# A decoder trunk planned by list scheduling: a denser layout for a small recursion, a higher threshold for constant products, and new priorities

## The chip, the core and the metric

The kernel runs on one core of one Trainium2 chip. A core has five engines that run side by side, each with its own instruction queue: TensorE (PE, matrix products; its weight loads are shown as PEld), VectorE (DVE), ScalarE (ACT), GpSimd (POOL) and SyncE (SP), which issues the transfers. The clock that TensorE is granted varies during a run, and the profile shows it. The metric is the device time of one execution in microseconds, as a median of several runs.

## The reference

A trunk of two layers over 512 positions of width 1024. Each layer is

```python
h = rms_norm(x, attn_pre_norm[i])
z = h @ w_in[i]
y_attn = dilated_attention_mixer(aq, ak, av, positions)
y_conv = conformer_conv_mixer(conv_u, conv_dw[i], ...)
y_gdn = gated_deltanet_mixer(gdn_qkv, gdn_gate, gdn_a, gdn_b, ...)
mix = jnp.concatenate([y_attn, y_conv, y_gdn], axis=-1)
x = x + rms_norm(mix @ w_out[i], attn_post_norm[i])
h = rms_norm(x, ffn_pre_norm[i])
f = (jax.nn.silu(h @ w_gate[i]) * (h @ w_up[i])) @ w_down[i]
x = x + rms_norm(f, ffn_post_norm[i])
```

What matters here is the gated DeltaNet with four heads of width 128. It works in chunks and solves, in each, a unit lower triangular system:

```python
m = jnp.where(strict, jnp.einsum('bhncd,bhnsd->bhncs', k_beta, k) * decay, 0.0)
sol = lax.linalg.triangular_solve(m + jnp.eye(C), rhs, left_side=True, lower=True, unit_diagonal=True)
```

## The kernel before

Activations lie transposed, features on the 128 partitions and the 512 positions along the row. Every large product (`dense`, line 703) is float32 split into two parts of a faster format: high times high, high times low, low times high, so three products of 512 (or twice 256) columns for each 128 x 128 block of weights. The weights come through SP in units of four blocks (tile `wr`) and are split into `wh` (ACT) and `wl` (DVE or POOL). The results of all these products are called `pmm`. There are 1600 blocks in all.

A layer's mixer is written as segments in the order of `SEGMENTS` (line 30): K, Q and V project and convolve the DeltaNet's keys, queries and values; C0, C1 and CN are the convolution module; A and B0 to B3 the attention; S the scan over chunks; G0 to G3 the output gates. Segment K also holds the triangular inverse. It forms the matrices `em` (named `am` in the code) for four heads by four blocks of 128 positions, cuts out the 16 x 16 blocks on the diagonal (`abd`, `acm`), and inverts all of these at once by a recursion over 16 columns (line 1059). For that, `acm` is negated (`acn`), written to a scratch array in HBM and read back with each row spread over 16 partitions (`aext`). Column c then takes, for each of two halves of the 16 matrices, one DVE product of c + 1 rows by 8 matrices (`sbt`) and one DVE reduction into `pext`: 32 products and 32 reductions a layer. From `pext` the block diagonal inverse `P` is made for each head, transposed by DVE in blocks of 32 (`tm`), and then merged to blocks of 32, 64 and 128 by small TensorE products: `pc`, `pd` and `pt` in the profile, with results moved by ACT and DVE in between (tile `c`).

No order is written by hand. The program first records all operations, each with a cost from a table (`cost`, line 252). `Plan.forward` (line 399) then simulates the engines and picks, at each free engine, the ready operation with the highest rank: the length of the longest path to the end, plus the segment's entry in `BONUS` (line 127), and for the matrix products of `dense` also that in `DENSE` (line 128), both in ns. An operation waits in `fits` (line 438) until the buffers that it needs are free, with caps: 78 slots of 512 columns in SBUF, 7 banks in PSUM, and quotas for single names (8 for `z`, the projected tiles). When TensorE has nothing ready, line 542 looks at the last `TICK` (3.41 us): if less work than `TUNE["fill"]`, in columns, was done, a product of constants, 256 columns, is put into TensorE's queue (tile `fill`, issued through line 1368). `TUNE["low"]`, 2900 columns, is the limit below which the planner believes that the clock halves. The resulting order is issued as it stands, so each engine's queue is fixed when the program is built. Most instructions carry the line of the helper that issues them, 591, so the profile is read by tiles.

Of the kernel before, what the change touches and what calls it, by code (L numbers as in the profile page):

```python
# [9 lines left out]
F32 = mybir.dt.float32  # L10
F32R = mybir.dt.float32r
AF = mybir.ActivationFunctionType
OP = mybir.AluOpType
# [116 lines left out]
TUNE = {'spread': 2.8, 'low': 2900, 'fill': 4000, 'warm': 12, 'early': 0, 'hib': 2000.0, 'raw': 4, 'half': 12000.0, 'taps': 14, 'plo': 4, 'hold': 1000, 'passes': 0, 'S': 78, 'P': 7, 'Q': 5, 'ahead': 5, 'more': 6, 'n_out': 4, 'n_ffn': 6, 'n_down': 2, 'n_in': 8}  # L130
# [112 lines left out]
class Plan:  # L243
# [8 lines left out]
    def cost(self, op, eng, name, outs, ins, kw):  # L252
# [24 lines left out]
        if eng == "DVE":  # L277
# [121 lines left out]
    def forward(self):  # L399
# [50 lines left out]
        while events:  # L450
# [17 lines left out]
            for e in engines:  # L468
# [4 lines left out]
                while avail[e] and (e != "SP" or len(skipped) < 12):  # L473
# [17 lines left out]
                    break  # L491
                if chosen:
# [101 lines left out]
def trunk(nc, tc, xT, wst, wab, par, con, big, out, depth=DEPTH, dbg=None):  # L594
# [4 lines left out]
    with ExitStack() as ctx:  # L599
# [202 lines left out]
        def project_out(k_tiles, gain, n_cut):  # L802

            o = [slot([128, S], name=f"o{m}") for m in range(KD)]
            acc = slot([128, S], name="oacc")
# [632 lines left out]
```

## Time and profile before

| what | value |
|---|---|
| median of 3 runs | 1375.4 us (1375.05 to 1376.79) |
| the profiled execution | 1378.01 us |
| its span, first to last instruction | 1376.2 us |
| mean granted TensorE clock | 0.981 |
| PE busy | 1340.8 us, 97% |
| DVE busy | 824.9 us, 60% |
| ACT busy | 650.8 us, 47% |
| POOL busy | 176.3 us, 13% |
| constant products (fill) | 109 |

The page gives busy times by engine, and then the span in 40 equal slices of 34.4 us, a digit of tenths for each. A row of instructions names the engine, the operation, the tiles (written <- read), the shapes, the count, and the busy time with the mean of one in ns. Matrix products overlap in the pipeline, so the time that one takes in a stream is read from start to next start. The rows on which the argument rests are shown in the prediction.

### The profile page before, as it was taken

The page shows a single profiled execution, that of the slowest core. Times are in us where ns is not written, and L with a number is a line of the kernel's source. Part 1 is how long each engine was busy: PE and PEld are TensorE (multiplying, and loading weights), DVE is VectorE, ACT ScalarE, POOL GpSimd, SP SyncE. Part 2 cuts the span into 40 slices and gives each one's busy share as a digit, 9 for nine tenths or more (in the row PEclk, how much of TensorE's full clock was granted, in tenths as well). Part 3 has the DMA queues.
Part 4 walks back from the last instruction along what each step waited for, and adds up shares of the span by engine and source line. Part 5 has one row for each costly group of instructions (what it writes and reads, how often), then busy time and mean ns, then how long its engine had stood idle before and what let it go on. Part 6 is the DMA issues. An engine that isn't in the chain of part 4 may idle for free.

```text
span 1376.2 us, 20826 instructions
## 1 busy us (share of the span) xinstructions
PE 1340.8 (97%) x7645; PEld 1143.7 (83%) x7645; DVE 824.9 (60%) x1739; ACT 650.8 (47%) x1523; POOL 176.3 (13%) x138
## 2 busy tenths in 40 slices
PE   8999999999999999999999899999999999999996
PEld 7977886798888888888998788777898888888886
DVE  7599889675343335533788848774493444346324
ACT  5565598864232224333574546796562222244321
POOL 1045562000000000000003347310000000000000
PEclk9999999999999999999999869999999999999998
DMA  6234121413333331432304113222232332223311
GB/s 244 63 68 135 51 62 32 146 55 92 100 94 90 92 92 47 123 106 85 108 16 100 39 55 90 79 62 77 84 110 86 105 92 85 87 57 114 111 46 62
DMA packets 64438, 118.51 MB, mean 86 GB/s; under 512 B 8016, under 2 KB 8784, under 8 KB 64336
## 3 DMA queue, kind: packets, MB, share of 16 engines
q1 hardware_dynamic: 64336, 117.19, 28.2%
q8 instruction: 60, 0.98, 0.3%
q14 instruction: 42, 0.34, 0.1%
HBM read 112.70 MB, written 2.36 MB: 84 GB/s over the span
## 4 chain that ended last, share of the span: by engine, by line
PE 83%; DVE 7%; ACT 6%; DMA 2%; issue 1%; SPq 1%; DVEq 0%; ACTq 0%
PE pmm L591 72%; PE pas L591 1%; PE pd L591 1%; PE pc L591 1%; PE pao L591 1%; DVE sct L591 1%; DMA wr<-in_wst_dram 1%; DVE sbt L591 1%; PE fill L1368 1%; SPq L591 1%; DVE wl L591 1%; PE pss L591 1%; ACT L588 1%; PE pbc L591 1%; DVE pext L591 1%
## 5 line engine op out<-in xcount | busy, mean ns | idle before, releaser
L591 DVE TENSOR_TENSOR wl<-wr,wh 128x512 fp32r<-128x512 f32 x382 | 265.3, 728 | 73.4 <-ACT wh L591 54.6
L591 ACT CAST wh<-wr 128x512 fp32r<-128x512 f32 x400 | 226.9, 619 | 48.9 <-PE pmm L591 30.6
L591 ACT ACTIVATE g<-g 128x512 f32<-128x512 f32 (+1 forms) x50 | 28.4, 579 | 303.9 <-DVE g L591 303.9
L591 DVE TENSOR_TENSOR g<-pmm,rst 128x512 f32<-128x512 f32 (+1 forms) x50 | 31.0, 626 | 216.2 <-PE pmm L591 215.8
L591 PE MATMUL pmm<-gl,wh 128*128 128x512 f32 (+1 forms) x440 | 124.9, 347 | 0.0
L591 PE MATMUL pmm<-gh,wl 128*128 128x512 f32 (+1 forms) x280 | 92.5, 347 | 0.0
L591 PE MATMUL pmm<-gh,wh 128*128 128x512 f32 (+1 forms) x280 | 92.3, 348 | 0.0
L591 PEld LDWEIGHTS pmm<-gl,wh 128*128 128x128 f32 x440 | 71.3, 189 | 10.5 <-DVE gl L591 0.4
L591 POOL TENSOR_TENSOR ca<-ca,cm 128x510 f32<-128x510 f32 (+12 forms) x52 | 69.3, 1333 | 30.8 <-ACT cm L591 26.7
L591 POOL TENSOR_TENSOR abd<-em,cn 128x512 f32<-128x512 f32 x8 | 10.1, 1292 | 488.4 <-PE pbc L591 483.7
L591 ACT ACTIVATE osq<-pmm 128x256 f32<-128x256 f32 (+1 forms) x40 | 18.8, 470 | 106.4 <-PE pmm L591 104.2
L591 PE MATMUL pmm<-h0h,wh 128*128 128x512 f32 (+1 forms) x168 | 62.0, 370 | 6.6 <-ACT h0h L591 5.0
L591 DVE TENSOR_TENSOR g<-pmm,g 128x512 f32<-128x512 f32 (+1 forms) x50 | 31.1, 625 | 57.3 <-PE pmm L591 55.7
L591 DVE TENSOR_TENSOR oacc<-oacc,osq 128x256 f32<-128x256 f32 (+1 forms) x36 | 19.1, 539 | 74.5 <-ACT osq L591 74.5
L591 PE MATMUL pmm<-h0h,wl 128*128 128x512 f32 (+1 forms) x168 | 60.4, 360 | 1.4 <-DVE wl L591 1.4
L591 DVE SCALAR_TENSOR_TENSOR ca<-cy,pr,ca 128x495 f32<-128x495 f32 (+8 forms) x64 | 60.1, 940 | 1.7 <-ACT ca L591 1.0
L591 PE MATMUL pmm<-h0l,wh 128*128 128x512 f32 (+1 forms) x168 | 61.0, 363 | 0.0
L591 PE MATMUL pmm<-h2h,wh 128*128 128x512 f32 (+1 forms) x168 | 60.2, 359 | 0.5 <-ACT h2h L591 0.5
L591 PE MATMUL pmm<-h6h,wh 128*128 128x512 f32 (+1 forms) x168 | 60.1, 360 | 0.5 <-ACT h6h L591 0.5
L591 PE MATMUL pmm<-h1h,wh 128*128 128x512 f32 (+1 forms) x168 | 60.4, 360 | 0.0
L591 PE MATMUL pmm<-h5h,wh 128*128 128x512 f32 (+1 forms) x168 | 59.8, 358 | 0.6 <-ACT h5h L591 0.6
L591 PE MATMUL pmm<-h7h,wh 128*128 128x512 f32 (+1 forms) x168 | 60.1, 358 | 0.2 <-ACT h7h L591 0.2
(410 smaller groups left out, 3784.1 us busy)
## 6 DMA issues: line engine op xcount, KB each, us to landing
wr<-in_wst_dram SPq DMA_DIRECT2D x400, 256.0 KB, 2.7
azs<-z SPq DMA_DIRECT2D x32, 64.0 KB, 2.0
out_dram<-x SPq DMA_DIRECT2D x8, 256.0 KB, 2.1
aext<-rows SPq DMA_DIRECT2D x16, 120.0 KB, 4.5
x<-in_xT_dram SPq DMA_DIRECT2D x3, 512.0 KB, 6.6
tab<-in_big_dram SPq DMA_DIRECT2D x6, 256.0 KB, 2.7
aext<-rows SPq DMA_DIRECT2D x16, 56.0 KB, 2.4
cn<-in_con_dram SPq DMA_DIRECT2D x1, 524.0 KB, 8.2
```

The source lines that it names most:

```text
L588: engines["ACT"].preload_act_table_set(TABLES[i])
L591: getattr(engines[op.eng], op.name)(*[real(v) for v in op.args], **{k: real(v) for k, v in op.kw.items()})
L1368: plan.fill = lambda pe: pe.matmul(spare, idr.real(), mkr.rearrange("p a b -> p (a b)").real(), start=True, stop=True)
```

## The change

Three things change in what is run.

First, the layout of `neg` and `aext`: the last two axes are exchanged, from 16 matrices by 8 columns to 8 columns by 16 matrices. The product `sbt` then reads eight neighbouring elements where it read eight elements with a step of 8. ACT writes `neg` with a step of 16 in place of neighbours.

Second, `TUNE["fill"]` goes from 4000 to 5500, and the planner's cost of a `tensor_reduce` from 1.042 to 1.8 ns an element.

Third, all entries of `BONUS` and `DENSE` are new; the order of the segments isn't.

The diff also adds a way to split the output projection (a segment "W", functions `partial` and `project_out` with `part`) and a threshold `force`. No segment of that name is in `SEGMENTS`, and `force` is 0.

```diff
-ORDER_MIX = [2, 3, 0, 1, 4, 5, 6, 7]
+MIX_FIRST, MIX_LAST = [2, 3, 0, 1], [4, 5, 6, 7]
...
-BONUS = [{'K': 7170.3, 'C1': -310689.2, 'Q': 2737.8, 'V': -21633.2, 'A': 377497.7, 'S': 500228.3, 'B3': 294757.3, 'G3': -170751.1, 'C0': -90236.6, 'CN': 57280.5, 'G1': -410936.0, 'B1': 116301.8, 'B2': -239277.2, 'G2': -907382.9, 'G0': -411196.1, 'B0': 106725.9}, {'K': 35258.6, 'Q': -73757.3, 'C1': -126597.0, 'V': -112818.6, 'S': 513179.7, 'C0': -100704.2, 'CN': 508090.7, 'A': 133320.4, 'G0': -505663.2, 'G3': 304870.7, 'G1': -924587.1, 'B1': -111116.6, 'G2': -647387.0, 'B2': 346444.4, 'B0': 9000.0, 'B3': -609034.4}]
-DENSE = [{'K': -47894.8, 'C1': 205847.3, 'Q': -11076.7, 'V': 6830.5, 'A': 116721.2, 'S': 29786.9, 'B3': 232625.1, 'G3': 125018.1, 'C0': 276368.0, 'CN': 50523.1, 'G1': -49707.6, 'B1': 5133.6, 'B2': -335640.4, 'G2': -74475.9, 'G0': 30693.3, 'B0': 57640.8}, {'K': -145783.0, 'Q': -251685.0, 'C1': 5059.7, 'V': 10117.4, 'S': -8457.8, 'C0': -6426.3, 'CN': -188413.0, 'A': -26229.6, 'G0': 62975.3, 'G3': -124736.2, 'G1': 56.4, 'B1': -20113.1, 'G2': 169737.3, 'B2': 136261.2, 'B0': 168289.6, 'B3': 107165.0}]
+BONUS = [{'K': 9227.4, 'C1': -623874.9, 'Q': 3537.5, 'V': -112716.9, 'A': 207529.5, 'S': 559775.1, 'B3': 222492.7, 'G3': -260564.1, 'C0': -342077.4, 'CN': 222956.7, 'G1': -470845.1, 'B1': -267748.8, 'B2': -155829.8, 'G2': -402814.4, 'G0': -13939.3, 'B0': -19819.2}, {'K': 201437.6, 'Q': -49423.7, 'C1': -132451.1, 'V': -106246.6, 'S': 471821.1, 'C0': -92812.5, 'CN': 667624.9, 'A': -207008.4, 'G0': -123094.8, 'G3': -644594.6, 'G1': -1342764.0, 'B1': 81040.5, 'G2': -837816.9, 'B2': 1003748.1, 'B0': 389050.4, 'B3': -625867.0}]
+DENSE = [{'K': 224813.1, 'C1': 391471.3, 'Q': 17335.8, 'V': -7374.5, 'A': 52394.6, 'S': 151271.5, 'B3': 61099.0, 'G3': 189334.6, 'C0': 532363.2, 'CN': -117887.5, 'G1': -418214.0, 'B1': 98270.2, 'B2': -230328.5, 'G2': -100662.5, 'G0': 302616.4, 'B0': -29981.7}, {'K': -7678.0, 'Q': -119981.2, 'C1': -2611.2, 'V': -11276.6, 'S': -238754.5, 'C0': 225389.9, 'CN': -313550.1, 'A': -168757.3, 'G0': 359195.8, 'G3': 144801.4, 'G1': 73170.5, 'B1': 329908.3, 'G2': 309427.5, 'B2': 231241.1, 'B0': -300255.7, 'B3': 148791.9}]
...
-TUNE = {'spread': 2.8, 'low': 2900, 'fill': 4000, ...
+TUNE = {'force': 0, 'spread': 2.8, 'low': 2900, 'fill': 5500, ...
...
+            if name == "tensor_reduce":
+                per = 1.8
...
+                if e == "PE" and TUNE["force"] and chosen and now > 30000 and ops[chosen[2]].work < 100:
...
-                    neg = slot([128, 2, 16, 8], name="acn")
-                    aext = bigs.tile([128, 24, 16, 8], F32, "aext")
+                    neg = slot([128, 2, 8, 16], name="acn")
+                    aext = bigs.tile([128, 24, 8, 16], F32, "aext")
...
-                        A.activation(neg[:, t], acm[:, :, :, 8 * t:8 * t + 8].rearrange("p h n c -> p (h n) c"), AF.Copy, scale=-1.0)
+                        A.activation(neg[:, t].rearrange("p c a -> p a c"),
+                                     acm[:, :, :, 8 * t:8 * t + 8].rearrange("p h n c -> p (h n) c"), AF.Copy, scale=-1.0)
...
-                        V.tensor_copy(aext[:, first], cn[:, d:d + 8].unsqueeze(1).to_broadcast([128, 16, 8]))
+                        V.tensor_copy(aext[:, first], cn[:, d:d + 8].unsqueeze(2).to_broadcast([128, 8, 16]))
...
-                            V.tensor_tensor(tmp[:, 0:c + 1], pext[:, 0:c + 1, a], aext[:, first:first + c + 1, a, c % 8], op=OP.mult)
+                            V.tensor_tensor(tmp[:, 0:c + 1], pext[:, 0:c + 1, a], aext[:, first:first + c + 1, c % 8, a], op=OP.mult)
...
+                if seg == "W":
+                    part = partial([mix[i] for i in MIX_FIRST])
...
-            update = project_out([mix[i] for i in ORDER_MIX], P(POST1, 8), TUNE["n_out"])
+            last = MIX_LAST if part else MIX_FIRST + MIX_LAST
+            update = project_out([mix[i] for i in last], P(POST1, 8), TUNE["n_out"], part)
```

More of the change, by code (lines that the diff above doesn't have):

```diff
@@ L129 @@
 QUOTA = {'pkt': 2, 'pso': 2, 'z': 8, 'cm': 2, 'pvt': 1, 'pkk': 2, 'pap': 1, 'as': 6, 'pas': 4, 'pks': 3, 'scm': 2, 'pqt': 1, 'pot': 2}
-TUNE = {'spread': 2.8, 'low': 2900, 'fill': 4000, 'warm': 12, 'early': 0, 'hib': 2000.0, 'raw': 4, 'half': 12000.0, 'taps': 14, 'plo': 4, 'hold': 1000, 'passes': 0, 'S': 78, 'P': 7, 'Q': 5, 'ahead': 5, 'more': 6, 'n_out': 4, 'n_ffn': 6, 'n_down': 2, 'n_in': 8}
+TUNE = {'force': 0, 'spread': 2.8, 'low': 2900, 'fill': 5500, 'warm': 12, 'early': 0, 'hib': 2000.0, 'raw': 4, 'half': 12000.0, 'taps': 14, 'plo': 4, 'hold': 1000, 'passes': 0, 'S': 78, 'P': 7, 'Q': 5, 'ahead': 5, 'more': 6, 'n_out': 4, 'n_ffn': 6, 'n_down': 2, 'n_in': 8}
@@ L491, in forward @@
                     break
+                if e == "PE" and TUNE["force"] and chosen and now > 30000 and ops[chosen[2]].work < 100:
+                    while recent and recent[0][0] < now - TICK:
+                        recent.pop(0)
+                    if sum(v for _, v in recent) < TUNE["force"]:
+                        skipped.append(chosen)
+                        chosen = None
                 if chosen:
@@ L800, in pre_norm, with partial, project_out @@
             return h, rst, last
-        def project_out(k_tiles, gain, n_cut):
+        def partial(k_tiles):
             o = [slot([128, S], name=f"o{m}") for m in range(KD)]
+            dense(k_tiles, KD, lambda i, cut, ps: A.copy(o[i], ps), FULL, ("pmm", TUNE["Q"]))
+            return o
+        def project_out(k_tiles, gain, n_cut, part=None):
+            o = part or [slot([128, S], name=f"o{m}") for m in range(KD)]
             acc = slot([128, S], name="oacc")
             def full(m, cut, ps):
-                A.activation(o[m], ps, AF.Copy, scale=gain[:, m:m + 1], **({"table": "n"} if m == 3 else {}))
+                set_ = {"table": "n"} if m == 3 else {}
+                if part:
+                    V.tensor_tensor(o[m], ps, o[m], op=OP.add)
+                    ps = o[m]
+                else:
+                    A.activation(o[m], ps, AF.Copy, scale=gain[:, m:m + 1], **set_)
+                    set_ = {}
                 if m == 0:
@@ L812, in full @@
                     sq = slot([128, S], name="osq")
-                    A.activation(sq, ps, AF.Square)
+                    A.activation(sq, ps, AF.Square, **set_)
                     V.tensor_tensor(acc, acc, sq, op=OP.add)
@@ L820, in half @@
                 sq = slot([128, S // 2], name="osq")
-                A.activation(sq, ps, AF.Square)
-                A.activation(o[m][:, cut], ps, AF.Copy, scale=gain[:, m:m + 1])
+                if part:
+                    V.tensor_tensor(o[m][:, cut], ps, o[m][:, cut], op=OP.add)
+                    A.activation(sq, o[m][:, cut], AF.Square)
+                else:
+                    A.activation(sq, ps, AF.Square)
+                    A.activation(o[m][:, cut], ps, AF.Copy, scale=gain[:, m:m + 1])
                 if m < KD - 1 or not cut.start:
@@ L885, in trunk @@
             cacc = [None, None]
+            part = None
             for seg in SEGMENTS[layer]:
@@ L1385, in layouts @@
     for i in range(DEPTH):
-        seq.append(blocks(f["w_in"][i], [c for c, _ in input_tiles(i)]))
-        wo = f["w_out"][i].reshape(KD, 128, D)[ORDER_MIX].reshape(D, D)
-        seq.append(blocks(wo, range(0, D, 128)))
+        wo = f["w_out"][i].reshape(KD, 128, D)
+        for name in SEGMENTS[i]:
+            if name == "W":
+                seq.append(blocks(wo[MIX_FIRST].reshape(-1, D), range(0, D, 128)))
+            else:
+                cols = [c for c, _ in COLUMNS.get(name, ())]
+                if cols:
+                    seq.append(blocks(f["w_in"][i], cols))
+        last = MIX_LAST if "W" in SEGMENTS[i] else MIX_FIRST + MIX_LAST
+        seq.append(blocks(wo[last].reshape(-1, D), range(0, D, 128)))
         gu = np.stack([blocks(f["w_gate"][i], range(0, HID, 128)).reshape(KH, KD, 128, 128),
```

9 lines of the change are left out of this document (6 added, 3 removed).

## The prediction

> **What bounds the kernel now.** I read the page first: the slices of the span and the chain of waits.
>
> ```profile
> span 1376.2 us, 20826 instructions
> ...
> PE   8999999999999999999999899999999999999996
> ...
> PEclk9999999999999999999999869999999999999998
> ...
> PE 83%; DVE 7%; ACT 6%; DMA 2%; issue 1%; SPq 1%; DVEq 0%; ACTq 0%
> ```
>
> TensorE is at nine tenths in nearly every slice and carries 83% of the chain: this is a TensorE-bound program, and a faster DVE or ACT instruction counts only where TensorE waits for it. The one place where both TensorE rows dip is slices 22 and 23, from 757 to 826 us, in the mixer of layer 1. So the second view is the busy time by windows there, cut where the granted clock changes.
>
> ```profile
> core 0: us, PE busy (x) PEld busy (x) DVE busy (x) ACT busy (x) POOL busy (x), PEclk, DMA share, GB/s
> 722.00:726.00 4.00, 3.73 (x18) 2.26 (x17) 3.84 (x18) 2.23 (x9) 0.11 (x1) 1.00 0.01 2
> 726.00:732.80 6.80, 6.80 (x31) 6.07 (x30) 5.17 (x8) 2.46 (x9) 6.41 (x6) 0.52 0.00 0
> ...
> 764.00:768.20 4.20, 4.20 (x20) 3.29 (x18) 4.20 (x15) 0.00 (x0) 0.10 (x1) 1.00 0.20 62
> 768.20:773.80 5.60, 0.17 (x1) 0.00 (x0) 5.60 (x10) 0.00 (x0) 0.00 (x0) 0.72 0.00 0
> 773.80:777.20 3.40, 3.36 (x16) 3.39 (x17) 3.40 (x7) 1.25 (x2) 0.00 (x0) 0.50 0.01 2
> 777.20:790.80 13.60, 12.54 (x145) 11.07 (x145) 10.44 (x22) 12.82 (x27) 9.15 (x8) 0.99 0.00 1
> 790.80:810.40 19.60, 19.60 (x177) 16.85 (x175) 8.85 (x18) 7.63 (x15) 10.35 (x10) 0.51 0.14 41
> 810.40:814.70 4.30, 4.30 (x11) 3.43 (x11) 1.79 (x3) 4.27 (x6) 2.55 (x3) 0.50 0.23 62
> ```
>
> The last three numbers of a row are the granted clock, the DMAs' share and GB/s. TensorE stands still for 5.6 us from 768.2, and in all it runs at half clock for 726.0 to 732.8, 773.8 to 777.2 and 790.8 to 814.7, in which it is recorded busy throughout. What it does there is told by the same view for single tiles: first the dense products (pmm), in two stretches of layer 0 and in this one, then the constant products (fill).
>
> ```profile
> 137.00:172.00 35.00, 20.81 (x79) 15.29 (x77) 2.01 (x3) 0.00 (x0) 0.95 0.17 53
> 172.00:206.00 34.00, 8.93 (x26) 4.24 (x26) 1.38 (x2) 0.00 (x0) 1.00 0.21 60
> ...
> 773.80:810.40 36.60, 0.01 (x1) 0.01 (x1) 1.36 (x2) 0.00 (x0) 0.69 0.08 23
> ```
>
> ```profile
> 773.80:790.80 17.00, 4.32 (x19) 3.29 (x19) 0.89 0.01 1
> 790.80:810.40 19.60, 8.06 (x24) 5.71 (x24) 0.51 0.14 41
> ```
>
> In layer 0 the small products that merge the 16-blocks (pc, pd, pt) run between dense ones. In layer 1 no dense product runs for 36.6 us: the merging products stand alone with 43 constant ones. I call 768.2 to 810.4, 42.2 us, the hole. The timeline of TensorE bounds it:
>
> ```profile
> 767.98 0.39 PE L591 MATMUL pmm<-h7l,wh 128*128 128x512 f32 x1
> 773.84 2.05 PE L591 MATMUL pc<-tm,a 128*128 128x128 f32 x8 [5.47 <-DVE tm L591]
> ...
> 786.11 1.09 PE L1368 MATMUL fill<-mkr,idr 128*128 128x256 f32 x7
> 787.13 0.69 PE L591 MATMUL pc<-tm,em 32*32 32x32 f32 x16
> ...
> 798.85 1.86 PE L1368 MATMUL fill<-mkr,idr 128*128 128x256 f32 x7
> 800.64 1.19 PE L591 MATMUL pd<-P,c 32*32 32x32 f32 x24
> ...
> 810.39 0.79 PE L591 MATMUL pmm<-h0h,wh 128*128 128x512 f32 x1
> ```
>
> From start to next start, seven constant products take 1.02 us at full clock (0.146 us each) and 1.79 us at half (0.256 us each).
>
> **The change part by part.** *What does nothing.* `force` is 0, so its test never holds. No segment is named W, so `part` stays None, MIX_FIRST + MIX_LAST is the old order, and the weights lie in the same sequence. Terms: 0.
>
> *Strideless rows.* The recursion's products (sbt, 32 a layer) read aext with a step of 8 elements before and of 1 after. Their rows and those of a dense one:
>
> ```profile
> L591 DVE TENSOR_TENSOR oacc<-oacc,osq 128x512 f32<-128x512 f32 x16 | 11.0, 690 | 50.9 <-ACT osq L591 50.9
> L591 DVE TENSOR_TENSOR oacc<-oacc,osq 128x256 f32<-128x256 f32 x20 | 8.1, 419 | 23.6 <-ACT osq L591 23.6
> ...
> L591 DVE TENSOR_TENSOR sbt<-pext,aext 128x128 f32<-128x128 f32 x4 | 1.4, 393 | 0.0
> L591 DVE TENSOR_REDUCE pext<-sbt 128x8 f32<-128x128 f32 x4 | 1.4, 380 | 0.0
> ...
> L591 DVE TENSOR_TENSOR sbt<-pext,aext 128x8 f32<-128x8 f32 x4 | 0.6, 167 | 0.0
> ...
> L591 DVE TENSOR_REDUCE acm<-abd 128x64 f32<-128x512 f32 x8 | 8.3, 1053 | 0.0
> ```
>
> Strided, an element costs (393 - 167) / 120 = 1.88 ns; dense, (690 - 419) / 256 = 1.06 ns. A layer has 2 x 8 x (1 + ... + 16) = 2176 elements, so 0.82 x 2176 = 1.8 us a layer if the step is the cause, 0 if something else in a small instruction is. I take 1.8, since the slope is read from the same instruction. The reductions (pext) keep their step and their time. The negated copy for the transfer (acn) and the constant row of aext get the step instead; each is at most a few instructions of 128 elements, 0.1 us by the slopes above, and off the chain or beside a transfer. The transfers have the same sizes. Where does the 1.8 us count? In layer 0 TensorE is at nine tenths in the slices of the recursion (2 and 3), so nothing. In layer 1 the DVE's timeline shows the recursion's end right ahead of TensorE's standstill:
>
> ```profile
> 767.51 0.70 DVE L591 TENSOR_TENSOR sbt<-pext,aext 128x128 f32<-128x128 f32 x2
> 768.14 0.66 DVE L591 TENSOR_REDUCE pext<-sbt 128x8 f32<-128x128 f32 x2
> 768.72 1.00 DVE L591 TENSOR_TENSOR P<-pext,cn 128x512 f32<-128x512 f32 x1
> 769.64 0.68 DVE L591 TENSOR_TENSOR wl<-wr,wh 128x512 fp32r<-128x512 f32 x1
> 770.24 2.83 DVE L591 TENSOR_TENSOR P<-pext,cn 128x512 f32<-128x512 f32 x3
> 773.00 0.69 DVE L591 STREAM_TRANSPOSE tm<-P 128x512 f32<-128x512 f32 x1
> ```
>
> All 1.8 us come off the 5.6 us. **Term: -1.8 us (0 to -1.8).** Late next is P, 3.8 us for four heads and in no part touched.
>
> *The planner's cost of a reduction.* It goes from 68 + 1.042 n to 68 + 1.8 n ns: for n = 128 from 201 to 298 (row: 380), for acm from 601 to 990 (row: 1053). Before, the planner saw this chain too short by 0.76 x 2176 for pext, as much again for the strided sbt (0.83 x 2176), and 0.76 x 512 x 4 for acm: 1.65 + 1.8 + 1.55 = 5.0 us, about the 5.6 us for which TensorE stands with neither dense nor constant products in its queue. Now the plan can put something there. A constant product there only saves the clock; a dense one saves the time. The rest of the idle is 3.8 us; I take half: **-2 us (0 to -3.8).**
>
> *Denser constant products.* Where the planner finds no product ready, it adds one of 256 columns while the last 3.41 us hold less than 5500 columns instead of 4000. At most that is 1500 / 256 = 5.9 more in each 3.41 us. Two effects. First the clock. 773.8 to 777.2 and 790.8 to 814.7 are 27.3 us at half clock with TensorE busy: at full clock they would last 13.65 us less if TensorE alone set the pace, and nothing less if the chain through DVE and ACT did (8.85 and 7.63 us busy in 19.6). The queue has the constant products to fill just those waits, so TensorE's side is nearer: I take two thirds, **-9 us (0 to -13.6).** The half clock at 726.0 I leave at 0: it follows 4 us with real products in TensorE's queue throughout, where none is added (end: -3.4). Second, their own time: in the 42.2 us, 12.4 x 5.9 = 73 more, 10.7 us at 0.146. At full clock the hole has room for them (next part: half of it is free), so only those count that stand just ahead of a product that has become ready: **+1.5 us (0 to +10.7).**
>
> The Trainium skill, page "TensorE: Matmul & The Clock Gate", Part 1, says that the clock halves after an idle window of about 3.4 us and returns after a busy one. The trace only half agrees: the clock halved at 773.8 behind 5.6 us of standstill, but again at 790.8, behind a stretch with 12.54 of 13.60 us recorded busy. Taken by that rule, more products in a stretch that is busy already would change nothing, and the sum would lose its 9 us.
>
> *New priorities.* BONUS and DENSE, added to the rank of each operation, are all new. Most of it is exchange among the stages of one mixer; layer 1's K, which holds this whole recursion, goes up by 166 us (35.3 to 201.4) and its dense products by 138 us, so the recursion should be passed by fewer other DVE steps, while V and C0, the dense work that could cover the merging products, move by under 9 us. No row prices an order that wasn't run. The bounds are this trace's two mixers: layer 1 loses about 21 us more in its hole than it needs (below), layer 0 has no such hole. So -21 to +21; nothing tells the sign for the rest: 0.
>
> Sum: -1.8 - 2 - 9 + 1.5 = -11.3 us. The profiled execution took 1378.0 us (span 1376.2 and 1.8 around it), 2.6 above the median of 1375.4. 1378.0 - 11.3 = 1366.7, scaled to the median 1364.
>
> **The rivals.**
> *The hole closes.* Dense products move between the merging ones, as in layer 0. The 43 constant products take 19 x 0.146 + 24 x 0.256 = 8.9 us; the merging ones 17.0 - 2.8 = 14.2 and, at half clock, 19.6 - 6.1 = 13.5, so 6.8 at full: 21 us of work in 42.2. Saved: 21 us and 2.1 of 810.4 to 814.7, so 1378.0 - 23 = 1355, about 1352. For it: K's bonus, and a planner that now sees the chain's length. Against it: V and C0 hardly moved.
>
> *The constant products don't hold the clock.* The 9 us stay lost, the 3.8 us of the two first terms come and the 1.5 us are paid: 1378.0 - 2.3 = 1375.7, by the median 1373, no change that can be told. For it: 790.8, where the clock fell though 19 had just been run. Against it: in the four stretches at full clock before and after, far more columns flow.
>
> *They hold it nowhere and are in the way (slower).* At 790.8 to 810.4 TensorE is busy all the time at half clock, so each further one is paid in full: 19.6 / 3.41 x 5.9 = 34 of them, at 0.256 us 8.7 us, less 3.8 gained: 1378.0 + 4.9, about 1380. It decides when the clock in the hole is still near 0.5 with over 60 constant products in it.
>
> *A second hole (slower).* Layer 0's cover (20.81 and 8.93 us of pmm in the rows above) is spent earlier or held back later by its new priorities, and its merging products stand alone too: +21 against the forecast, about 1384. It decides when pmm in that stage falls below 10 us. Against it: C1 and V of layer 0 go down (by 313 and 91 us), which leaves dense work for later.
>
> **How the numbers follow.** Forecast 0.50 (own range 1356 to 1371), hole closes 0.17, clock not held 0.11, in the way 0.09, second hole 0.13. A measurement of this kernel can tell about 0.2% (2.8 us) from no change. Faster than 1372.6: 0.50 + 0.17 = 0.67; same 0.11; slower 0.22. The range leaves out the best half of the closed hole and the worse half of the second one: 1348 to 1383.
>
> **What would show it.** Right: sbt of 128 elements near 300 ns, with pext still near 380; in layer 1, between the last dense product ahead of the first pc and the next dense one, a granted clock above 0.9; no standstill of 5 us ahead of the first pc; well over 109 constant products, none of them the cause of a wait. The clock of the whole span above 0.981. Wrong: the clock in the merging stretch at 0.5 to 0.7 with more constant products in it; or layer 0 showing a stretch of over 20 us with no pmm; or layer 1 showing none, with a gain above 20 us.

## The result: slower by 0.9%, with a second hole in layer 0

The changed kernel takes 1388.45 us (median of 4 runs, 1387.64 to 1390.18) beside 1375.91 us for the kernel before in the same job (4 runs, 1375.05 to 1376.79): a ratio of 1.009, with a 95% interval of 1.0076 to 1.0105. The forecast was 1364.0 us in a range of 1348.0 to 1383.0. The slower rival "a second hole", with 1384, came closest, and even it lies under the result.

The page of the changed kernel: the span, the busy times and TensorE's clock by slices:

```profile
span 1385.9 us, 21158 instructions
...
PE 1356.8 (98%) x7825; PEld 1162.9 (84%) x7825; DVE 810.5 (58%) x1739; ACT 650.7 (47%) x1521; POOL 174.0 (13%) x138
...
PEclk9999999999999999999999979999999999999998
```

Read alone, this page looks better than the one before: TensorE is busier, the clock lost only in one slice instead of two, the mean clock 0.985 instead of 0.981. But 180 more instructions on TensorE (7825) are constant products, 289 instead of 109. Busy time that holds constant products says nothing of the work done, so the dense products have to be looked at alone. They are compared in layer 0's mixer, by windows, first in the kernel before:

```profile
206.00:223.60 17.60, 11.09 (x43) 7.78 (x43) 0.00 (x0) 0.00 (x0) 1.00 0.17 53
223.60:240.80 17.20, 1.96 (x5) 0.78 (x5) 2.02 (x3) 0.00 (x0) 1.00 0.06 17
240.80:258.00 17.20, 9.06 (x33) 5.62 (x33) 0.69 (x1) 0.00 (x0) 1.00 0.51 155
258.00:272.00 14.00, 14.00 (x63) 11.54 (x62) 0.00 (x0) 2.46 (x4) 1.00 0.49 146
```

and then in the changed one (the columns are the window and its length, the busy time of pmm on TensorE and of its weight loads, the steps of DVE and ACT that read or write pmm, then clock, DMA share, GB/s):

```profile
172.00:206.00 34.00, 24.99 (x93) 16.30 (x91) 2.06 (x3) 0.00 (x0) 1.00 0.20 63
206.00:223.60 17.60, 7.42 (x26) 4.53 (x26) 0.00 (x0) 0.00 (x0) 1.00 0.35 106
223.60:240.80 17.20, 2.83 (x11) 1.99 (x11) 1.36 (x2) 0.00 (x0) 1.00 0.10 31
240.80:258.00 17.20, 0.00 (x0) 0.00 (x0) 0.68 (x1) 0.00 (x0) 1.00 0.29 86
258.00:272.00 14.00, 0.77 (x3) 0.67 (x4) 0.00 (x0) 0.00 (x0) 1.00 0.35 104
```

Between 172 and 206 us the changed kernel runs 24.99 us of dense products where the one before ran 8.93. Between 240.8 and 272 it has 0.77 us left where the one before had 23.06. The kernel before has a hole here too, a shorter one: 1.96 us of dense products in the 17.2 us from 223.6.

These windows alone say too much, though. The same view from 69 us on adds them up: for the kernel before up to 206 us and up to its output projection, and then for the changed one:

```profile
69.00:206.00 137.00, 91.03 (x362) 67.44 (x362) 9.89 (x15) 0.00 (x0) 0.99 0.28 79
69.00:255.90 186.90, 111.11 (x434) 80.06 (x434) 12.26 (x19) 0.00 (x0) 0.99 0.27 76
```

```profile
69.00:206.00 137.00, 99.93 (x419) 73.95 (x419) 10.46 (x16) 0.00 (x0) 1.00 0.29 82
69.00:271.20 202.20, 110.18 (x456) 80.46 (x456) 12.50 (x19) 0.00 (x0) 1.00 0.29 81
```

By 206 us the changed kernel is 8.9 us of dense work ahead and not 16, since at 172 us it was behind (74.94 us against 82.10). And both kernels have done the same dense work, 110 to 111 us, when the output projection starts: at 256.0 us in the kernel before, at 271.2 in the changed one. So most of the 23.06 us is the output projection itself, and what the changed kernel loses is its later start.

TensorE's timeline shows what stands ahead of that start:

```profile
262.95 5.87 PE L1400 MATMUL fill<-mkr,idr 128*128 128x256 f32 x47
271.23 0.50 PE L599 MATMUL pmm<-mch,wh 128*128 128x512 f32 x1 [2.41 <-ACT mch L599]
```

Forty-seven constant products in a row, then 2.41 us of standstill, and the dense work goes on when ACT has written mch, the convolution's part of the mix. In the kernel before the first output product with mch ran at 256.0 us.

To put one number on each mixer I took, from the trace, every product's time from start to next start at full clock (the median of its shape), left the constant products out, and called the rest of the time lost to TensorE:

| lost, us | up to 275 us | up to 688 us | 688 to 1101 us |
|---|---|---|---|
| before | 25.6 | 33.1 | 48.1 |
| after | 43.1 | 49.8 | 42.4 |

Layer 0's mixer loses 17.5 us more, layer 1's 5.7 us less. Layer 0's excess is 16.7 us at 688, so the two together are 11.0, against 9.7 us between the spans. The figures depend on which products are counted as one shape: other groupings move them by several us, and the differences between kernels by up to 4.

In layer 1 the hole is still there. All engines by windows in the changed kernel (the first two overlap), after the end of the dense products at 783 us:

```profile
787.30:794.10 6.80, 6.28 (x28) 5.99 (x29) 5.21 (x11) 3.31 (x5) 1.09 (x1) 0.50 0.00 0
791.00:808.00 17.00, 17.00 (x191) 15.08 (x191) 11.82 (x26) 13.97 (x30) 9.97 (x9) 0.90 0.01 1
808.00:828.00 20.00, 20.00 (x147) 17.59 (x146) 10.49 (x19) 8.18 (x13) 9.30 (x7) 0.50 0.17 54
```

The last stretch runs at half clock with TensorE recorded busy throughout, just as 790.8 to 810.4 did before. In all TensorE is at half clock for 27.3 us here (6.8 from 787.4 and 20.5 from 807.8), as long as the prediction counted in the kernel before.

### The profile page after: what moved, and what is told of

It reads as the page before. It is cut to its first block, busy times and chain, and to the rows that moved or that the text cites. A ratio compares the mean times of both kernels' runs of the same rounds, so it can differ in the third digit from the quotient of the medians.

```text
span 1385.9 us, 21158 instructions
## 1 busy us (share of the span) xinstructions
PE 1356.8 (98%) x7825; PEld 1162.9 (84%) x7825; DVE 810.5 (58%) x1739; ACT 650.7 (47%) x1521; POOL 174.0 (13%) x138
## 4 chain that ended last, share of the span: by engine, by line
PE 86%; DVE 5%; ACT 5%; issue 2%; DMA 1%; SPq 0%; DVEq 0%; ACTq 0%
PE pmm L599 73%; PE fill L1400 2%; PE pd L599 1%; PE pc L599 1%; PE pas L599 1%; PE pbc L599 1%; PE pao L599 1%; PE pss L599 1%; ACT junk L599 1%; PE pso L599 1%; DVE wl L599 1%; ACT wh L599 1%; DVE pext L599 1%; ACT L596 1%; DVE sbt L599 1%
## 5 line engine op out<-in xcount | busy, mean ns | idle before, releaser
L599 DVE TENSOR_TENSOR wl<-wr,wh 128x512 fp32r<-128x512 f32 x382 | 260.8, 715 | 92.5 <-ACT wh L599 71.6
L599 ACT CAST wh<-wr 128x512 fp32r<-128x512 f32 x400 | 227.5, 619 | 46.2 <-PE pmm L599 27.3
L599 DVE SCALAR_TENSOR_TENSOR ca<-cy,pr,ca 128x497 f32<-128x497 f32 (+7 forms) x64 | 62.8, 982 | 2.4 <-ACT ca L599 1.8
L599 PE MATMUL pmm<-h3h,wh 128*128 128x512 f32 (+1 forms) x168 | 60.4, 361 | 0.0
L599 PE MATMUL pmm<-h2l,wh 128*128 128x512 f32 (+1 forms) x168 | 60.1, 358 | 0.0
L599 PE MATMUL pmm<-h2h,wl 128*128 128x512 f32 (+1 forms) x168 | 60.1, 359 | 0.0
## 6 DMA issues: line engine op xcount, KB each, us to landing
wr<-in_wst_dram SPq DMA_DIRECT2D x400, 256.0 KB, 2.7
out_dram<-x SPq DMA_DIRECT2D x8, 256.0 KB, 2.1
tab<-in_big_dram SPq DMA_DIRECT2D x6, 256.0 KB, 5.0
```

Of the source, the lines that this page charges most:

```text
L599: getattr(engines[op.eng], op.name)(*[real(v) for v in op.args], **{k: real(v) for k, v in op.kw.items()})
```

## The experiments

The leading theory, after the result: **layer 0's new priorities spend the dense products too early, and nothing is left to cover the scan and the attention.** The rivals: the new layout costs time, the constant products are in the way, or the gain in layer 1 was never to be had. Ratios are to the kernel before on the same chip, with 95% intervals.

**1. The layout alone.** The new layout of the recursion's rows, and nothing else of the change, in the kernel before.

```diff
-V.tensor_tensor(tmp[:, 0:c + 1], pext[:, 0:c + 1, a], aext[:, first:first + c + 1, a, c % 8], op=OP.mult)
+V.tensor_tensor(tmp[:, 0:c + 1], pext[:, 0:c + 1, a], aext[:, first:first + c + 1, c % 8, a], op=OP.mult)
...
```

> The kernel before with the new layout of neg and aext alone; the planner's costs don't see the difference, so its order stays. If the step of 8 elements is what made the recursion's products slow, one of 128 elements takes about 300 ns in place of 393, and the 1.8 us of layer 1 come off TensorE's standstill ahead of the first merging product (5.6 us): 0.998 to 0.999 of the time before. If the recursion isn't what TensorE waits for, or the writing of neg with a step costs as much, 1.000.

Measured: 0.9975 (0.996 to 0.999). The groups of its recursion by form:

```profile
L591 DVE TENSOR_REDUCE pext<-sbt 128x8 f32<-128x128 f32 x4 | 1.4, 386 | 0.0
L591 DVE TENSOR_TENSOR sbt<-pext,aext 128x128 f32<-128x128 f32 x4 | 1.0, 280 | 0.0
L591 DVE TENSOR_TENSOR sbt<-pext,aext 128x8 f32<-128x8 f32 x4 | 0.6, 158 | 0.0
```

and the row of its tile acn (shortest, median and longest in ns, first and last start):

```profile
L591 ACT ACTIVATE acn<-acm x4: 429/432/433, 85.8 to 736.1; 128x128 f32<-128x128 f32 x4
```

The product of 128 elements went from 393 to 280 ns, the reduction stayed. The layout is a gain, not the loss. And part of it lies where it was predicted: TensorE's standstill ahead of the first pc of layer 1 was 5.47 us before and is

```profile
769.75 1.13 PE L591 MATMUL pc<-tm,a 128*128 128x128 f32 x8 [3.63 <-DVE tm L591]
```

here, 1.84 us less. The copy acn is looked at below.

**2. The change with layer 0's old priorities.** Layer 1 keeps the new ones.

```diff
-BONUS = [{'K': 9227.4, 'C1': -623874.9, ...}, {'K': 201437.6, ...}]
+BONUS = [{'K': 7170.3, 'C1': -310689.2, ...}, {'K': 201437.6, ...}]
...
```

> The changed kernel with layer 0's BONUS and DENSE of before; layout, threshold 5500, reduction cost and layer 1's priorities stay new. Theory (layer 0's new priorities end its mixer with a stretch of no dense product, 223 to 271 us): layer 0 is again about 17 us shorter, so about 1371, below the kernel before. Rival (the denser constant products stand in the way): their number stays well over 109 and the time stays near 1385. Second rival (any change of the priorities makes the plan lose, wherever it is): over 1380 with the loss in another place.

Measured: 0.9959 (0.9943 to 0.9974), 1372.12 us. Layer 0's priorities alone are worth 1.009 - 0.9959 = 1.3% or some 18 us, all of the loss and more. The dense products by windows in this kernel:

```profile
172.00:206.00 34.00, 7.47 (x21) 3.61 (x21) 1.38 (x2) 0.00 (x0) 0.85 0.11 34
...
240.80:258.00 17.20, 9.07 (x35) 6.48 (x36) 0.69 (x1) 0.00 (x0) 1.00 0.54 169
258.00:272.00 14.00, 13.44 (x71) 11.32 (x69) 0.69 (x1) 0.00 (x0) 1.00 0.26 78
```

The dense products lie as in the kernel before, 7.47 us in 172 to 206 and 22.51 in 240.8 to 272, and the output projection starts at 254.2 us. This is the lowest ratio of the study, though its interval overlaps those of 1, 4 and 11.

**3. The change without constant products.** The order is the same, and `fill` issues nothing. What is left out are products whose results nobody reads.

```diff
-plan.fill = lambda pe: pe.matmul(spare, ...)
+plan.fill = lambda pe: None
```

> The changed kernel with its order kept as it stands and every constant product left out (289 fewer small products, whose results nothing reads). Theory (they only fill waits): the clock falls in the long waits of layer 0 and in the hole, and the time rises by 5 to 20 us, to 1394 to 1409. Rival (they stand in the way): the time falls by several us, to 1375 to 1385.

Measured: 1.011 (1.0081 to 1.0138), 1393.09 us, mean clock 0.968. Beside the change's 1.009 (1.0076 to 1.0105) the intervals overlap: 289 constant products raise the clock from 0.968 to 0.985, and the time hardly tells of it. As a whole they don't make the loss.

But the sum hides two effects. In layer 0 the constant products help: without them mch is written at 281.8 us, 11.2 us later than in the change. In layer 1 they are in the way. These are all engines from the first pc to the next dense product, in the change and then without constant products:

```profile
787.24:823.30 36.06, 35.54 (x336) 31.88 (x336) 21.70 (x48) 21.16 (x40) 14.65 (x12) 0.69 0.08 24
```

```profile
798.31:827.43 29.12, 26.22 (x289) 23.80 (x289) 21.65 (x48) 21.38 (x40) 14.92 (x12) 0.68 0.10 28
```

The order, the work of DVE and ACT and the clock are the same, and the stretch is 6.9 us shorter without its 48 constant products (one profiled execution each). A version that keeps them in layer 0 alone was not run.

**4. The kernel before with each constant product issued twice.** Nothing else is changed.

```diff
-plan.fill = lambda pe: pe.matmul(spare, ...)
+plan.fill = lambda pe: [pe.matmul(spare, ...) for _ in range(2)]
```

> The kernel before with its order kept and each of its 109 constant products issued twice. If the prediction's 9 us term holds (the clock in layer 1's merging stretch is held by more columns, and TensorE sets the pace there), the granted clock at 790 to 815 us is near 1 and the time falls by 6 to 12 us, to 1364 to 1370. If the constant products only lengthen a saturated stretch, the clock stays at 0.5 there and the time rises by 24 x 0.256 = 6 us, to about 1382.

Measured: 0.9978 (0.9964 to 0.9993). The same two stretches of layer 1 as in the prediction's windows:

```profile
773.80:790.80 17.00, 16.36 (x152) 15.22 (x152) 13.55 (x29) 12.70 (x24) 7.71 (x7) 0.87 0.00 1
790.80:810.40 19.60, 19.48 (x230) 17.25 (x231) 9.90 (x22) 9.77 (x20) 12.46 (x11) 0.91 0.19 50
```

The clock of the second stretch goes from 0.51 to 0.91. The time gains about 3 us (0.22% of 1376, interval 1.0 to 5.0), where two thirds of the half-clock time were to give 9. So the clock was held, and most of the gain wasn't there. What took it shows in the stretch up to the next dense product, first the constant products, then the longest waits (who waited for whom, us in total, times, longest):

```profile
790.80:808.60 17.80, 9.91 (x54) 7.98 (x54) 0.90 0.14 36
```

```profile
ACT c L591 <- PE pc L591: 9.6, 4, 7.4
DVE P L591 <- PE pd L591: 5.9, 5, 2.5
```

TensorE doesn't wait for DVE and ACT here, they wait for its merging products, and 9.91 of its 17.80 us are constant products. So twice as many of them stand in the way, as in 3. How much of the missing 6 us that is was not measured apart.

**5. Only C1's bonus back.** The change, with one number of layer 0 as before.

```diff
-'C1': -623874.9
+'C1': -310689.2
```

> The changed kernel with one number of before: layer 0's BONUS of C1, -310689 in place of -623875, so that the first half of the convolution is planned earlier. Theory (layer 0's late convolution leaves VectorE idle between 69 and 206 us and overloaded behind it, where no dense product is left for TensorE): VectorE is busier before 206 us than in the changed kernel (109.7 of 137 us), the stretch without dense products is shorter, and the time falls by 5 to 12 us, to about 1378 to 1385 on a scale where the changed kernel takes 1.009 of before. Rival (the loss is in the attention's or the gates' priorities): within 3 us of the changed kernel.

Measured: 1.0006 (0.9986 to 1.0026). One entry of 32 takes back nearly all of the 0.9%. But it doesn't bring the dense products back: it runs 24.70 us of them in 172 to 206, like the change, and 10.77 in 258 to 272, since its output projection starts at 264.7 instead of 271.2. (Its profiled execution took 1383.83 us, 3.45 more than its median of 1380.38, so the trace shows it at its worse end: up to 275 us it loses only about 4 us less than the change, and where the rest of the gain lies isn't shown.) VectorE's busy time over 69 to 206 us, which I had thought would come back to the 126 us of the kernel before, stayed at 105.7 (the change: 109.7). The mechanism that I had behind this experiment, a VectorE that idles early and is late at the end, was thereby in doubt.

**6 and 7. Without VectorE's convolution taps in layer 0, change and before.** The order is kept. What is left out are the 32 tap instructions of layer 0 on VectorE, so the convolution is incomplete.

```diff
 op = self.ops[i]
+if op.eng == "DVE" and op.i < len(self.ops) // 2 and op.name == "scalar_tensor_tensor" and op.args[1].buf.name == "cy":
+    continue
```

> The changed kernel in its own order with a part of the computation left out: VectorE's 32 convolution taps of layer 0 (29.0 us of VectorE, the last ends at 250 us). Theory (VectorE's late convolution ends layer 0's mixer): the first product of the output projection starts 10 to 17 us earlier than at 271 us, and the time falls by as much, to about 1372 to 1380. Rival (attention's chain through ScalarE sets that end): it starts less than 5 us earlier, since the last attention rows come at 264 us.

> The kernel before in its own order with the same part left out: VectorE's 32 convolution taps of layer 0 (29.6 us, the last ends at 231 us). There the convolution isn't what ends the mixer, so by the theory the time falls by less than 6 us, to over 0.996 of before; the contrast to the same cut in the changed kernel is what counts. By the rival both fall alike.

Measured: 1.0083 (1.0058 to 1.0109) for the change and 0.9991 (0.9977 to 1.0006) for before. With 25 us of VectorE's work gone (810.5 to 785.2), the change's first output product starts at 273.0 us, not earlier. The theory "VectorE's late convolution ends layer 0's mixer" fell.

**8. Merging products limited to two PSUM banks, in the kernel before.** The rival "the hole closes" as an experiment: with fewer of the seven banks held by merging products, dense ones can run between them.

```diff
 def bank(shape=(128, S), name="pb"):
-    return banks.tile(shape, F32, name)
+    t = banks.tile(shape, F32, name)
+    if name in ("pc1", "pd1", "pc2", "pd2", "pt3", "pc3", "pd3"):
+        t.buf.quota = ("merge", 2)
+    return t
```

> The kernel before with the merging products held to two PSUM banks at a time, so that dense products find banks among them; the planner orders anew. In its list of TensorE's instructions 48 dense products stand between the first and the last merging product of layer 1 in place of none. If the prediction's second case is right (dense products in the hole save up to 21 us), the time falls by over 8 us, to under 1368. If the merging chain itself gets as much longer as the dense products take (48 x 0.227 = 10.9 us), or layer 0 pays for the same limit, it stays within 6 us of before or rises.

Measured: 1.0077 (1.0043 to 1.0111), span 1383.8 us. Its dense products and its clock in layer 1, where the kernel before had none for 36.6 us:

```profile
780.00:800.00 20.00, 5.33 (x21) 3.43 (x20) 1.35 (x2) 0.00 (x0) 0.83 0.03 7
800.00:826.00 26.00, 11.79 (x36) 6.29 (x37) 0.67 (x1) 0.00 (x0) 1.00 0.17 50
```

The hole did close, with 17.1 us of dense products and the clock at 0.83 and 1.00. By the accounting above, 757 to 826 us loses 18.2 us instead of 26.8, but the stages behind give half of it back, and the whole of layer 1's mixer loses 43.7 instead of 48.1: 4.4 us gained, not 21. Layer 0, under the same limit, gets a second hole of its own and loses 17.6 us more up to 688 us (50.7 against 33.1). That fits a stock of dense work, where what is spent in one place is missing in the next.

**9 and 10. Priorities and settings, crossed.** The change with both layers' old priorities, and the kernel before with both layers' new ones.

```diff
-BONUS = [...]  # and DENSE
+BONUS = [...]  # those of the other kernel
```

> The changed kernel with both layers' BONUS and DENSE of before; layout, threshold 5500 and the reduction's cost stay new. If the new priorities are bad by themselves, this is faster than the changed kernel, under 1.004 of before. If priorities fit only the settings that they were found for, so that either half alone falls apart, it is slower than the changed kernel: over 1.015 of before, with over 300 constant products in stretches that lack dense ones.

> The kernel before with the new BONUS and DENSE alone: old layout, threshold 4000, old cost of a reduction. If the new priorities carry the whole loss, about the changed kernel's 1.009. If they fit only the new settings, over 1.02 of before.

Measured: 1.0242 (1.0214 to 1.0271) and 1.0289 (1.0262 to 1.0316). Both are worse than either kernel. The old priorities under the new settings lose nothing in layer 0 (33.9 us up to 688) but 81.7 us in layer 1, against 48.1. The new ones under the old settings lose 60.5 us up to 688, against 33.1, and in layer 1 a few us more, for which the accounting is too coarse. So layer 1's old priorities don't fit the new settings, and layer 0's new ones lose still more under the old settings than under the new (60.5 against 49.8). It isn't a rule for all of them: layer 0's old priorities did well under both.

**11 and 12. Gains put together.** The kernel before with the new layout and constant products twice (11), and kernel 2 with constant products twice (12).

```diff
...
+plan.fill = lambda pe: [pe.matmul(spare, ...) for _ in range(2)]
```

> The order of the kernel before, the new layout, and each constant product issued twice: the two gains of e1 (0.9975) and e4 (0.9978) together. If they lie in different stretches (the standstill ahead of the merging products, and the half clock in them), they add up to 0.995. If the merging stretch is one chain and one gain eats the other, 0.997 to 0.998.

> The kernel of e2 (layer 0's priorities of before, all else changed, 0.9959) with each of its 177 constant products issued twice. It has half clock at 168 to 182, 773 to 779 and 790 to 814 us, 44 us in all. By e4's size (20 us less of half clock gave 3 us) it gains 2 to 5 us more: 0.992 to 0.995. If the constant products, now twice as many, start to stand ahead of real ones, 0.996 or more.

Measured: 0.9972 (0.9951 to 0.9993) and 0.9984 (0.997 to 0.9999). Whether the gains of 1 and 4 add is left open: their sum would be 0.9953, inside the interval. 2 gains nothing more from a clock of 0.992.

**13 to 16. What sets the end of the second hole?** ScalarE is busy 32.05 of 34.4 us from 223.6 to 258 in the change, so it was the next suspect. At fixed order, these leave out layer 0's 16 scalings of the normalized heads (13, and 14 in before), all but the first taps of layer 0's convolution on VectorE, ScalarE and GpSimd (15), and both (16).

```diff
+if early and op.eng == "ACT" and name.startswith("ot") and args[1].buf is args[0].buf:  # 13, 14, 16
+    continue
+if early and (op.eng == "DVE" and op.name == "scalar_tensor_tensor" and op.args[1].buf.name == "cy"
+              or name == "cm" or op.eng == "POOL" and ... op.args[2].buf.name == "cm"):  # 15, 16
+    continue
```

> The kernel after in its own order, without the 16 scalings of the gates' input in layer 0 (ACT ot<-ot,ro, 128x128, 0.394 us each, 6.3 us, all between 206 and 240 us). What it leaves out: the output norm of the DeltaNet's heads in layer 0. The order is unchanged. Theory 'ScalarE's queue ends layer 0's mixer': it is busy 32.05 of the 34.4 us before 258, so the last exponentials, csq and mch move up by 5 to 6 us, the first output projection starts near 266 instead of 271.2, and the time falls by 4 to 6 us: 1.005 to 1.006 of before. Rival 'the chain through TensorE, VectorE and ScalarE of the attention and of the convolution's norm ends it, whatever ScalarE's load': under 1.5 us, 1.008 to 1.009.

> The same 16 scalings left out of the kernel before, order unchanged: the control. Output projection starts at 256.0 in before. By the theory ScalarE's queue moves up here too (it is busy 32.63 of 34.4 us), but dense products cover until 265 us, so at most 2 us are gained: 0.9985 to 1. By the rival nothing: 1.

> The kernel after in its own order, without all of layer 0's convolution taps but the first two: the 32 on VectorE, the 26 products on ScalarE (cm) and their 26 additions on GpSimd. What it leaves out is most of the convolution of layer 0. Only the first projections and the join, the norm and the activation stay. Theory 'ScalarE's queue': 7 of the cm lie behind 206 us, 5 us of ScalarE, and 19 before, so first output product 4 to 6 us earlier than 271.2, 1.004 to 1.006. Theory 'the convolution's taps on ScalarE and GpSimd are late': the join of the two sums no longer waits, same or more. Rival 'the order in the queues alone': the join still stands behind the attention in VectorE's queue, under 1.5 us, 1.008 to 1.009.

> Both left out at once (the scalings, and the convolution's taps on all three engines, in layer 0), after's order. Theory 'ScalarE's queue': 11 us less for ScalarE behind 206 us, first output product near 261, and the second hole closes for the most part: 1.001 to 1.003. Rivals: 1.007 to 1.009.

Measured: 1.0057 (1.003 to 1.0083), 0.9991 (0.9972 to 1.0011), 1.0052 (1.0035 to 1.007) and 1.0059 (1.0037 to 1.0082). 13, 15 and 16 lie 0.3 to 0.4% under the change's 1.009, only 15 with an interval that doesn't meet the change's, so this load is a part of the loss, and a smaller one; 15 and 16 have no control in the kernel before. The runs of 16 lie between 1379.53 and 1391.32 us, wider than the effects, so the places in the trace have to tell the rest. Of 13, the two casts of mch (ns, then the first and last start):

```profile
L604 ACT CAST mch<-cvo x2: 615/616/616, 270.1 to 270.6; 128x512 fp32r<-128x512 f32 x2
```

Of 15, the same with the attention's score products (pas) and the sum of the convolution's halves (csum):

```profile
L604 ACT CAST mch<-cvo x2: 614/615/616, 268.8 to 269.3; 128x512 fp32r<-128x512 f32 x2
L604 PE MATMUL pas<-azc x32: 272/481/693, 222.8 to 247.3; 64*128 64x512 f32 x8, 64*128 64x128 f32 x8, 64*128 64x384 f32 x8, 64*128 64x256 f32 x8
L604 POOL TENSOR_TENSOR csum<-ca,ca x1: 1272/1272/1272, 249.6 to 249.6; 128x512 f32<-128x512 f32 x1
```

And the same three of the change and, below, of before:

```profile
L599 ACT CAST mch<-cvo x2: 614/615/616, 270.6 to 271.1; 128x512 fp32r<-128x512 f32 x2
L599 PE MATMUL pas<-azc x32: 272/481/693, 222.6 to 249.1; 64*128 64x512 f32 x8, 64*128 64x128 f32 x8, 64*128 64x384 f32 x8, 64*128 64x256 f32 x8
L599 POOL TENSOR_TENSOR csum<-ca,ca x1: 1278/1278/1278, 252.2 to 252.2; 128x512 f32<-128x512 f32 x1
```

```profile
L591 ACT CAST mch<-cvo x2: 599/608/616, 255.3 to 256.3; 128x512 fp32r<-128x512 f32 x2
L591 PE MATMUL pas<-azc x32: 272/481/693, 215.3 to 242.7; 64*128 64x512 f32 x8, 64*128 64x256 f32 x8, 64*128 64x128 f32 x8, 64*128 64x384 f32 x8
L591 POOL TENSOR_TENSOR csum<-ca,ca x1: 1272/1272/1272, 231.9 to 231.9; 128x512 f32<-128x512 f32 x1
```

6.3 us less on ScalarE move mch by 0.5 us; nearly the whole convolution less moves it by 1.8; both (16) by 3.7, to 266.9. So neither ScalarE's load nor the taps set most of the 15.3 us by which mch is later than in before. The sum of the convolution comes at 249.6 us although its taps are gone, 17.7 us later than in before, and the attention's first product stays at 222.8. What is left is the order of the queues. The join of the convolution, the step of VectorE that csum waits for (ca<-ca,ca), stands right behind an instruction of the attention in VectorE's queue, here in 15:

```profile
248.33 0.42 DVE L604 CUSTOM_DVE_ANT_0 as<-pas,tab 128x256 f32<-128x256 f32 x1
...
248.74 0.68 DVE L604 TENSOR_TENSOR ca<-ca,ca 128x512 f32<-128x512 f32 x1
```

and the attention starts 7.3 us later than in before. At a fixed order that couldn't be moved, so the last two runs changed it.

**17 and 18. The attention's or the convolution's priorities back.** The change, with layer 0's entries of A and B0 to B3 (17), or of C0, C1 and CN (18), as in before.

```diff
-'A': 207529.5, 'B0': -19819.2, ...     # 17, BONUS; DENSE likewise
+'A': 377497.7, 'B0': 106725.9, ...
-'C1': -623874.9, 'C0': -342077.4, 'CN': 222956.7     # 18, BONUS; DENSE likewise
+'C1': -310689.2, 'C0': -90236.6, 'CN': 57280.5
```

> The kernel after, with the BONUS and DENSE entries of layer 0's A and B0 to B3 (the attention) as in before; all else as after, order planned anew. Theory 'the attention starts late': its first product (pas) starts at 222.6 us in after and at 215.3 in before, and no work left out of ScalarE, VectorE or GpSimd moved that. With the old entries it starts by 217, the first output product comes by 263 instead of 271.2, and the time is 1.000 to 1.004 of before. Rival 'the ranks of the convolution against the rest': the start moves, the join of the convolution and its norm stay last behind 250 us, 1.007 to 1.010. Third: the layers' entries only fit together, 1.01 or more.

> The kernel after, with the BONUS and DENSE entries of layer 0's C0, C1 and CN (the convolution) as in before; all else as after. Theory 'the attention starts late': no better than with C1's BONUS alone (1.0006), since its attention started at 228.2: 1.000 to 1.006. Rival 'the ranks of the convolution against the rest': the join comes before 235 us as in before (231), dense products are left for 229 to 265, and the time is 0.996 to 0.999. Third: 1.01 or more.

Measured: 1.0094 (1.0075 to 1.0113) and 1.0058 (1.0035 to 1.008). With the attention's old entries its products start even later, at 226.2 us. With the convolution's, csum comes at 243.8 and mch at 265.0, but the attention ends later (mah at 278.0). The dense products of 18:

```profile
172.00:206.00 34.00, 26.36 (x100) 17.75 (x98) 2.74 (x4) 0.00 (x0) 1.00 0.25 69
...
240.80:258.00 17.20, 0.00 (x0) 0.00 (x0) 0.00 (x0) 0.00 (x0) 1.00 0.21 57
```

Neither group alone makes the hole. In the changed kernel, 5, 17 and 18 alike, 24 to 26 us of dense products run from 172 to 206 us (17: 24.25), and none is left at 240.8 to 258. With all of layer 0's old entries (2) it is 7.47 us, and dense products are left behind. **Shown:** the loss is layer 0's new priorities (2); its form is an output projection that starts 15.3 us later, behind 44 us (from 226.8) without dense products; neither VectorE's taps, nor the load that was taken off ScalarE and GpSimd, set most of that. **Not shown:** the leading theory itself, that dense products run too early. They go with the hole, but all of the mixer's dense products come ahead of the output projection in either kernel, and 5 spends them as early as the change and still measures 1.0006. What is late in the changed kernel is the convolution's chain behind csum (252.2 against 231.9 us). **Open:** which entries make it late. C1's bonus has the largest part of those tried (5); K, Q, V, S and G0 to G3 were not run. K's DENSE, from -47.9 to +224.8 us, would draw dense products forward by its sign.

## Why the prediction was wrong

**The bound: right, and not enough.** The time is set where TensorE lacks dense products; I looked for such a place only in layer 1. Layer 0 had one as well, from 223.6 to 240.8 us, behind the two windows that I read.

**Strideless rows: right in mechanism, under in size.** Expected were sbt of 128 elements at about 300 ns with pext still near 380: 280 and 386. The term of -1.8 us measured -3.4 us (0.25% of 1376, interval 1.4 to 5.5), so 1.8 lies inside, and the standstill ahead of the first pc became 1.84 us shorter. The acn copy, which writes with the step now, costs 432 ns instead of 302, 0.13 us each, beside the 0.1 that was allowed.

**The planner's reduction cost: right in place, without a gain.** The standstill of 5.6 us ahead of the first merging product became 14 constant products and 2.4 us of standstill; TensorE's timeline of the changed kernel has both:

```profile
782.81 0.39 PE L599 MATMUL pmm<-h7l,wh 128*128 128x512 f32 x1
783.03 1.83 PE L1400 MATMUL fill<-mkr,idr 128*128 128x256 f32 x14
787.24 1.95 PE L599 MATMUL pc<-tm,a 128*128 128x128 f32 x8 [2.38 <-DVE tm L599]
```

Not a dense one is among them, so by the prediction's own words this could save only the clock, and it didn't: 787.30 to 794.10 runs at 0.50. (In the kernel before the clock had fallen inside the standstill: its row has 0.72 for 768.2 to 773.8, so it was not 773.8 where it halved.) Its -2 us isn't separable from the priorities that were found with it (9 and 10).

**Denser constant products, -9 us and +1.5 us: both mis-sized.** In the changed kernel 808 to 828 us still runs at 0.50, so the threshold of 5500 did not hold the clock, and nothing of the 9 us was earned: 27.3 us at half clock as before. Where the clock is held (4: 0.91), the gain is 3 us, and in that stretch over half of TensorE's time is constant products. Their own time was the term that was far too small: 1.5 us were taken, and 3 measures 6.9 us for all those of layer 1's merging stage. So the rival "the constant products don't hold the clock" was right on the clock. "They are in the way" was right for layer 1, where the mechanism is the one that it names, and wrong for the whole, since in layer 0 the constant products save more than that. "TensorE's side is nearer" stands: DVE and ACT waited for TensorE in that stretch.

The Trainium skill, page "TensorE: Matmul & The Clock Gate", Part 1, has the clock fall after an idle window and return after a busy one. The trace does not bear out recorded busy time as its measure: 808 to 828 us was busy 20.00 of 20.00 us at 0.50, and in 4 a stretch busy 19.48 of 19.60 with 230 products instead of 177 had 0.91.

**New priorities, 0: the step that failed.** "The bounds are this trace's two mixers ... nothing tells the sign for the rest: 0" put nothing on the one part that moved the time by 1.3%, and gave no reason but that no row told its sign. The bound of +21 was good: layer 0 lost 17.5 us more. Layer 1 gained 5.7 in the change (8.1 in 2: 40.0 us lost from 688 to 1101 against 48.1), of which the layout alone gives 3.1 (45.0 in 1). The text against the second hole was the wrong way round: "C1 and V of layer 0 go down, which leaves dense work for later" took a lower rank for a gain. C1 holds the convolution, whose result the output projection takes first; with C1 back alone the loss shrinks from 0.9% to 0.06%. It also read BONUS alone, though the rank of a dense product has DENSE added: with both, those of C1 and V in layer 0 go down by 128 and 105 us, those of K up by 275, and layer 1's C0, said to move by under 9 us, goes up by 240. And the place was wrong: the rival was to be read by pmm below 10 us in the merging stage, where it rose from 8.93 to 24.99; the hole opened one stage later.

**The hole closes, 21 us: refuted as priced.** With the hole closed in 8, layer 1 gained 4.4 us. A hole of 42 us that holds 21 us of work isn't worth 21 us where the dense products that would fill it are needed by the stage behind.

**The range.** Its upper end of 1383.0 left the worse half of the second hole out. With the whole of that rival (1384) and the 9 us that were not earned, the range would have held the result.

## What to carry to other kernels

Where independent work hides a latency-bound chain, count that work as a stock: for each stage write down how much the plan spends and how much the next stage still needs, before pricing a hole at its width. Add the stock up from a common start and not by single windows, and note when the chain begins that releases the next stage. New ranks of a list scheduler are no exchange with a sum of zero; treat them as the largest term, with the range of the worst mixer seen, and try them layer by layer, since here one layer's gained and the other's lost. And products that only keep the clock up have a price of their own: leave them all out once, and look at each stage by itself, since here they saved 11 us in one and cost 7 in another while the total stood still.

## What the runs showed of the hardware

- A DVE product of two float32 operands took (393 - 167) / 120 = 1.88 ns an element with an operand read at a step of 8 elements, and (280 - 158) / 120 = 1.02 without.
- An ACT copy of 128 x 128 float32 took 302 ns writing densely and 432 to 438 ns writing with a step of 16 elements.
- TensorE's granted clock halved in stretches where it was recorded busy throughout (20.00 of 20.00 us at 0.50), and stood at 0.91 with 230 products where 177 had left it at 0.51 (19.48 and 19.60 us busy of 19.60).
- A stretch with the same work on DVE and ACT and the same clock (0.69 and 0.68) took 36.06 us with 48 constant products in TensorE's queue and 29.12 without.
